# Token sums built in the down inputs' tiles, padding tiles of 160 and 352 bytes, and quarter weights that begin 480 bytes into longer tiles

## The chip, the cores and the metric

The kernel runs on one core of one Trainium2 chip. The metric is the device time of one execution in microseconds (us), the median over several runs. Before the change the median of 3 runs is 1138.71 us (1138.31 to 1138.89).

The engines of a core are named as the profile names them: PE is TensorE, the matrix engine (PEld is its loading of weights, which overlaps the matmuls); DVE is VectorE; ACT is ScalarE; POOL is GpSimd; SP is the engine that issues most of the transfers here. SBUF is the on-chip memory of 128 partitions from which PE reads both operands of a matmul: the *stationary* operand (the weights, 128 x 128) and the *moving* operand (128 partitions by 256 or 512 columns, one column after the other). PSUM is the memory that holds its results.

## The reference

A decoder trunk of two layers on 512 tokens of width 1024, in float32. Layer 0 mixes the tokens with a gated delta rule in 6 heads, layer 1 with sliding-window attention in 12 heads; both also attend to 256 memory tokens with 4 heads. Each layer then has an output projection and a SwiGLU feed-forward part of width 2816. Cut to what matters:

```python
for layer in range(DEPTH):                       # 2 layers
    h = rms_norm(x, ln_mix[layer])
    ...                                          # memory keys and values; mixer of the layer; queries mem_q
    mem_o = memory_attention(mem_q, mem_k, mem_v)
    x = x + jnp.concatenate([mix_out, mem_o], axis=-1) @ w_out[layer]
    x = x + swiglu(rms_norm(x, ln_ffn[layer]), w_gate_up[layer], w_down[layer])
    ...                                          # after layer 0: the K and V shared by layer 1
return rms_norm(x, ln_final)

def swiglu(h, w_gate_up, w_down):
    gu = h @ w_gate_up                           # 512 x 1024 times 1024 x 5632
    return (jax.nn.silu(gu[..., :D_FF]) * gu[..., D_FF:]) @ w_down
```

## The kernel before

Everything is held transposed: 128 features on the partitions, the 512 tokens (T) along a row, so that the 1024 features are 8 tiles (KD). P is 128, D is 1024, T is 512, and a float32 has 4 bytes.

**Products.** A float32 product is made of three matmuls of a faster type, float32r. Each operand is split into a high part, which ACT copies (`copy`, L140), and a low part, which DVE subtracts (`tt`, L153; `split` calls both). `mm3` then issues, for one 128 x 128 block of weights, high by high, high weight by low input, and low weight by high input (all L146). In the profile a group such as `pj<-ac8l,whi` reads: into PSUM tile `pj`, from moving operand `ac8l` and stationary operand `whi`.

**Weights.** `weight` loads a block of up to 128 x 1024 into a tile `wraw` by SP (L179) and splits it into a pair `whi`, `wlo` of the pool `wpool`, three pairs in turn. The tiles are all [P, D], that is 4096 bytes in each partition.

**The feed-forward part** (`ffn`) has 22 blocks of 128 hidden features in two halves of 11. The first blocks of a half are computed directly: `gate`, `projected`, with 512-column matmuls. The other gate and up products go in pairs of blocks through `quarters`: the 2 x 2 block product of Strassen's kind in Winograd's form with 7 products in place of 8, each of 12 matmuls of 256 columns. Of the 84 matmuls of one such step 48 have as moving operand a sum of quarters of the input (tiles `T`, groups `g<-T,whi` and `g<-T,wlo`) and 36 a quarter of the input itself (`g<-h,...`, `g<-l,whi`). There are 38 steps: 19 in each layer. Each product takes the next place of `ring`: a half of one of the three `whi`/`wlo` pairs, 512 elements.

**The sums.** `token_sums` makes the sums for `quarters`, four calls in each layer (j = 0 to 3) while the first gates run. A call computes four 128 x 256 sums with DVE (L1251 and L156) into one tile `raw` [P, D] and splits it through `weight` into two of eight tiles `T` [P, D], with one ACT and one DVE instruction over 1024 columns.

**Down.** After 11 hidden blocks their activations (8 pairs `h`, `l` of another pool, and 3 pairs `ac8` to `ac10` of the pool `fp`) are multiplied by the down weights, 33 matmuls of 512 columns for each of 8 output tiles (a *row*). In the second half of layer 1 the last two rows are taken in halves of 256 tokens (the *tail*), and the weights of the last one then lie in `T` tiles.

**Attention parts.** `mq0`, `mq1` are the pairs that hold the output of the memory attention of layer 0, and are the moving operand of 48 matmuls in its output projection. `oh`, `ol` are weights of the output projection of layer 1 (the *own* weights), loaded early into a pool of its attention `sp`; 48 matmuls use them.

**Where tiles lie.** Each pool hands out addresses in the order in which its tiles are first asked for, so a tile put in between moves those behind it. The kernel writes down no addresses; they follow from sizes and order. The order of instructions on each engine is set by a scheduler from the data and buffers that each waits for.

Of the kernel before, what the change touches and what calls it, by code (L numbers as in the profile page):

```python
# [9 lines left out]
F32 = mybir.dt.float32  # L10
F32R = mybir.dt.float32r
# [7 lines left out]
P = 128  # L19
T = 512  # L20
D = 1024
# [6 lines left out]
FT = DFF // P  # L28
# [58 lines left out]
class Builder:  # L87
# [94 lines left out]
    def weight(self, src, eng=None, raw=None, parts=1, pool=None, tags=("whi", "wlo"), bufs=3, after=None):  # L182

        raw = self.load(src) if raw is None else raw
        n = raw.shape[1]
        hi = self.t(pool or self.wpool, [P, D], F32R, tags[0], bufs)[:, :n]
        lo = self.t(pool or self.wpool, [P, D], F32R, tags[1], bufs)[:, :n]
        for i in range(parts):
            s = slice(i * n // parts, (i + 1) * n // parts)
            self.split(raw[:, s], hi[:, s], lo[:, s], eng or self.weng)  # L190
            if after is not None:
                for ins, other in zip((self.copied, self.low), after):
                    self.nosync(ins, other)
        return hi, lo

    def mm3(self, ps, w, k, act, start, stop, more=False):

        (wh, wl), (ah, al) = w, act
        s = slice(k * P, (k + 1) * P)
        self.head = self.mm(ps, wh[:, s], ah, start, False, more)  # L200
        self.mm(ps, wh[:, s], al, False, False, more)
        self.last = self.mm(ps, wl[:, s], ah, False, stop, more)
# [289 lines left out]
    def gates(self, ep):  # L492
        nc, a = self.nc, self.a
        ab = self.t(ep, [P, T], F32, "ab")
        self.copy(ab, self.ab)
        pt = self.bank("g")
        sel = self.consts[:, C_SEL:C_SEL + 12]
        for c in range(NC):
            self.mm(pt[:, c * 12:(c + 1) * 12], ab[:, c * P:(c + 1) * P], sel)
        pv = pt[:, 0:48].rearrange("p (c e) -> p e c", e=12)  # L500
        z = self.t(ep, [P, 12, NC], F32, "z")
        self.copy(z[:, 0:H, :], pv[:, 0:H, :])
        self.tt(nc.vector, z[:, H:, :], pv[:, H:, :],
                self.small[:, 6:12].unsqueeze(2).to_broadcast([P, H, NC]), ALU.add)
        l = self.t(ep, [P, 12, NC], F32, "l")
        self.stt(l, z, -1.0, z, ALU.mult, ALU.max)
        self.fn(l, l, AF.Exp, scale=-1.0)
        self.softplus = self.fn(l, l, AF.Ln, bias=self.one)

        self.lnb = self.t(self.mpool, [P, H, NC], F32, "lnb")  # L510
        self.stt(self.lnb, z[:, 0:H, :], 0.0, l[:, 0:H, :], ALU.min, ALU.subtract)
        ea = self.t(ep, [P, H], F32, "ea")
        self.fn(ea, self.small[:, 0:6], AF.Exp)
        g = self.gate[:, :NH].rearrange("p (h c) -> p h c", c=NC)
        self.stt(g, z[:, H:, :], 0.0, l[:, H:, :], ALU.max, ALU.add)
        self.stt(g, g, -1.0, ea.unsqueeze(2).to_broadcast([P, H, NC]), ALU.mult, ALU.mult)
        g2 = self.gate[:, :NH]
        pg = self.bank("g")
        self.mm(pg[:, 64:64 + P], self.gate, self.U)
        self.mm(pg[:, 0:NH], self.U, g2)  # L520
        self.mm(pg[:, NH:2 * NH], self.ones, g2)
        row = self.t(ep, [NH, P], F32, "row")
        self.copy(row, pg[:NH, 64:64 + P])
        dr = self.t(self.dpool, [1, NH * P], F32, "dr")
        nc.sync.dma_start(dr.rearrange("o (n i) -> (o n) i", i=P), row)
        self.dr = dr
        self.ngc = self.t(self.mpool, [P, NH], F32, "ngc")
        self.ts(self.ngc, pg[:, 0:NH], -1.0, ALU.mult)
        self.negc = self.t(self.mpool, [P, NH], F32, "negc")
        self.fn(self.negc, pg[:, 0:NH], AF.Exp)  # L530
        self.ts(self.negc, self.negc, -1.0, ALU.mult)
        self.egl = self.t(self.mpool, [P, NH], F32, "egl")
        self.fn(self.egl, pg[:, NH:2 * NH], AF.Exp)
        self.glc = self.t(self.mpool, [P, NH], F32, "glc")
        self.tt(nc.vector, self.glc, pg[:, NH:2 * NH], self.ngc, ALU.add)
# [15 lines left out]
    def gdn(self, gp):  # L551
# [56 lines left out]
        f = self.t(gp, [P, 3, NH], F32, "f")  # L608
# [10 lines left out]
        for h in range(H):  # L619
            d = DT[h]  # L620
            for c in range(NC):
                i = h * NC + c
# [18 lines left out]
        def memory_queries(m):  # L641
            mq.append(self.pair(self.mpool, f"mq{m}"))
            qm.append(self.t(self.mpool, [P, T], F32, f"qm{m}"))
            self.copy(qm[m], self.normed(4 * H + m))

        for h in range(H):
            t = self.t(gp, [P, T], F32, "qv", 5)
# [7 lines left out]
        self.use(LN_EXP)  # L655
        scores = [self.scores(gp, qm[0], self.memK[0], False)]
        memory_queries(1)
        X, every_t = self.base_inverse(gp, base_in, known)
        Tt = [every_t[:, h * NC:(h + 1) * NC, :] for h in range(H)]
# [434 lines left out]
    def ffn(self, fp, xp, layer, h, apool, rope=False):  # L1094
# [1 line left out]
        nc, a = self.nc, self.a  # L1096
        acc = self.acc
        half = FT // 2
        acts, sums, open_pairs, places, waiting = [], [], [], [], []

        col = lambda f, up: a["wgu"][layer, 2 * f + up]

# [14 lines left out]

        def put(u):
            n = len(acts)
            acts.append(self.pair(apool) if n < KD else self.pair(fp, f"ac{n}"))  # L1120
            self.split(u, *acts[-1])

        def ring():

            if not places:
                for _ in range(3):
                    two = [self.t(self.wpool, [P, D], F32R, t, 3) for t in ("whi", "wlo")]
                    places.extend(tuple(x[:, i * T:(i + 1) * T] for x in two) for i in range(2))
            places.append(places.pop(0))
            return places[-1]  # L1130

        def begin(f, up, by, tag, bufs, then):

            o = [self.t(fp, [P, T], F32, tag, bufs) for _ in range(2)]
            steps = self.quarters(fp, [col(f + i, up) for i in range(2)], sums, by, o, ring)
            next(steps)
            while waiting:
                x = waiting.pop()
                self.nosync(self.fn(x, x, AF.Silu), self.held)
            end()  # L1140
            next(steps)
            open_pairs.append((steps, then, o))
            return o

        def end():
            if open_pairs:
                steps, then, o = open_pairs.pop()
                next(steps, None)
                for x in o:
                    then(x)  # L1150
# [8 lines left out]
        for f0 in (0, half):  # L1159
# [4 lines left out]
            u = self.t(fp, [P, T], F32, "fu", 3)  # L1164
            self.tt(nc.vector, u, list(up)[-1], g, ALU.mult)
            put(u)
            for f in range(f0 + 1, f0 + half, 2):
                if f == 1:
# [26 lines left out]
        if tail < KD:  # L1195
# [9 lines left out]
            for t in parts:  # L1205
                acc = self.acc[:, t]
                for m in range(tail, KD):
                    ps, x = self.bank("pj")[:, :T // 2], self.x[m][:, t]
# [6 lines left out]
                    if seeded:  # L1215
                        x = ps
# [21 lines left out]
    def token_sums(self, fp, layer, j, h):  # L1238


        nc, q = self.nc, T // 2
        if j == 0:
            self.minus = self.t(fp, [P, 4], F32, "minus")
            self.ts(self.minus, self.gains[:, G_FFN[layer] + 4:G_FFN[layer] + 8], -1.0, ALU.mult)
        g0, g1 = (self.gain(G_FFN[layer], j + i) for i in (0, 4))
        n1 = self.minus[:, j:j + 1]
        x0, x1 = self.x[j], self.x[j + 4]
        c = self.t(fp, [P, q], F32, "fc")
        raw = self.t(fp, [P, D], F32, "raw")
        t = [raw[:, i * q:(i + 1) * q] for i in range(4)]  # L1250
        ins = nc.vector.tensor_scalar(out=c, in0=x0[:, q:], scalar1=g0, scalar2=None, op0=ALU.mult).ins  # L1251
        if layer and j:

            self.nosync(ins, self.ended)
        self.stt(t[0], x0[:, :q], g0, c, ALU.mult, ALU.subtract)
        self.stt(t[1], x1[:, q:], n1, t[0], ALU.mult, ALU.subtract)
        self.stt(t[2], x1[:, q:], g1, c, ALU.mult, ALU.subtract)
        self.stt(t[3], x1[:, :q], n1, t[1], ALU.mult, ALU.subtract)
        hl = self.weight(None, raw=raw, pool=fp, tags=("T", "T"), bufs=8)
        parts = {f"t{i + 1}": [x[:, i * q:(i + 1) * q] for x in hl] for i in range(4)}  # L1260
        parts["11"] = [x[:, :q] for x in h[j]]
        parts["21"], parts["22"] = ([x[:, i * q:(i + 1) * q] for x in h[j + 4]] for i in range(2))
        return parts
# [123 lines left out]
    def swa(self, sp):  # L1387
# [97 lines left out]
        for t in range(6):  # L1485
            score(t)
            work, n = (queries(t + 2), (2, 3, 4)) if t < 4 else (rows[t - 4], (1, 1, 2))
# [8 lines left out]
        settle(*beside(5, some(rows[3], 2), some(rows[4], 3), (next(rows[m]) for m in (4, 4, 4, 0, 1))))  # L1496
        for m in range(2, 5):
            list(some(rows[m], 1))
        return mix, rows

    def final(self, fp, acc, x, o, t, width):
# [105 lines left out]
```

## Time and profile before

| | before |
|---|---|
| median of 3 runs | 1138.71 us (1138.31 to 1138.89) |
| the profiled execution | 1139.05 us |
| its span | 1136.9 us |
| granted TensorE clock, mean | 0.998 |
| PE busy | 1127.1 us (99%), 7339 matmuls |
| DVE busy | 828.7 us (73%), 1545 instructions |
| ACT busy | 635.1 us (56%), 1277 instructions |
| POOL busy | 73.1 us (6%), 91 instructions |

The span runs from the first to the last instruction that the profiler saw; the execution's own time is 2.15 us longer. Where two matmuls follow each other without a wait, the second one starts before the end of the first is recorded, so durations overlap; what a matmul costs is the distance from its start to the start of the next one. A timeline row gives the start, the duration, the engine and the instruction, and `x2` stands for two neighbours of one kind in one row. In the groups the columns after the bar are the busy time of the group in us and the mean of one instruction in ns.

The stages that matter below, by the start times of their matmuls in the profiled execution: output projection of layer 0 up to 318.7 us; feed-forward part of layer 0 with quarter products at 318.7 to 406.8 and 479.6 to 577.6 us, and down rows at 406.8 to 474 and 577.6 to 644 us; projections and attention of layer 1 to 767 us, its output rows to 783 us; first gates of its feed-forward part to 805.7 us, quarter products to 893.7 and from 966 to 1064.5 us, down rows at 893.7 to 961 and 1064.5 to 1114 us; the tail to 1127 us, and the last store.

### The profile page before, as it was taken

To read this page: it belongs to the slowest core of one execution; us is meant where nothing else is said; L and a number is where in the kernel's file an instruction comes from. 1 tells how busy PE (TensorE), PEld (TensorE's weight loads), DVE (VectorE), ACT (ScalarE), POOL (GpSimd) and SP (SyncE) were. 2 spreads that over 40 slices of the span, in tenths; PEclk is the share of its full clock that TensorE was granted. 3 is DMA by queue.
4 is the path that set the end of the run, shared out by engine and by line. 5 is a ranking of instruction groups with operands and counts; after the bars stand their busy time and mean duration, and the time that the engine had idled before them with its cause. 6 is when DMAs were issued, how large, how long until landed. Compare 5 with 4: busy or idle time off the path is not lost.

```text
span 1136.9 us, 19317 instructions
## 1 busy us (share of the span) xinstructions
PE 1127.1 (99%) x7339; PEld 991.7 (87%) x7339; DVE 828.7 (73%) x1545; ACT 635.1 (56%) x1277; POOL 73.1 (6%) x91
## 2 busy tenths in 40 slices
PE   9999999999999999999999999999999999999997
PEld 8888778887899988899988887788999988999986
DVE  7676976577888975588955877839999533889643
ACT  8588664566566632366643555956666322666434
POOL 0000000000011001011000000000112000111000
PEclk9999999999999999999999999999999999999999
DMA  8344252234567536377533321116587533676232
GB/s 312 112 149 149 93 130 85 84 121 148 172 162 189 140 108 176 102 179 193 135 88 102 130 74 38 56 39 191 147 195 188 142 101 105 172 190 155 77 102 86
DMA packets 72399, 151.14 MB, mean 133 GB/s; under 512 B 16956, under 2 KB 18516, under 8 KB 72308
## 3 DMA queue, kind: packets, MB, share of 16 engines
q1 hardware_dynamic: 60884, 129.21, 36.0%
q0 software_dynamic: 11136, 20.45, 11.0%
q8 instruction: 57, 0.93, 0.3%
q14 instruction: 34, 0.28, 0.1%
q10 hardware_dynamic: 288, 0.26, 0.1%
HBM read 142.94 MB, written 6.96 MB: 132 GB/s over the span
## 4 chain that ended last, share of the span: by engine, by line
PE 96%; DVE 2%; ACT 1%; DMA 0%; issue 0%; SPq 0%; DVEq 0%; ACTq 0%
PE pj L146 46%; PE g L146 38%; PE sc L146 6%; PE qk L146 3%; PE pt L146 2%; PE pt L150 1%; PE g L150 1%; DVE big L153 1%; DMA early<-in_early 0%; DVE qv L156 0%; DVE btmp L153 0%; DVE wlo L153 0%; ACT sm L134 0%; ACT whi L140 0%; DVE T L153 0%
## 5 line engine op out<-in xcount | busy, mean ns | idle before, releaser
L140 ACT ACTIVATE whi<-wraw 128x512 fp32r<-128x512 f32 (+3 forms) x318 | 235.8, 749 | 254.1 <-PE pj L146 170.5
L153 DVE TENSOR_TENSOR wlo<-wraw,whi 128x512 fp32r<-128x512 f32 (+3 forms) x318 | 263.5, 839 | 92.3 <-ACT whi L140 84.7
L146 PE MATMUL pj<-h,whi 128*128 128x512 f32 (+1 forms) x652 | 256.4, 395 | 0.0
L146 PE MATMUL pj<-l,whi 128*128 128x512 f32 (+1 forms) x652 | 254.4, 390 | 0.0
L146 PE MATMUL pj<-h,wlo 128*128 128x512 f32 (+1 forms) x652 | 254.0, 390 | 0.0
L146 PE MATMUL g<-T,whi 128*128 128x256 f32 x1216 | 218.5, 280 | 0.0
L146 PEld LDWEIGHTS g<-T,whi 128*128 128x128 f32 x1216 | 186.1, 188 | 1.2 <-DVE fu L156 1.2
L146 PE MATMUL g<-T,wlo 128*128 128x256 f32 x608 | 170.1, 280 | 0.0
L146 PEld LDWEIGHTS pj<-h,whi 128*128 128x128 f32 x652 | 122.4, 188 | 28.2 <-issue 4.1
L146 PE MATMUL g<-h,wlo 128*128 128x256 f32 (+1 forms) x500 | 146.1, 292 | 0.0
L146 PE MATMUL g<-l,whi 128*128 128x256 f32 (+1 forms) x500 | 146.0, 292 | 0.0
L146 PE MATMUL g<-h,whi 128*128 128x256 f32 (+1 forms) x500 | 145.6, 291 | 0.0
L146 PEld LDWEIGHTS pj<-h,wlo 128*128 128x128 f32 x652 | 122.5, 188 | 25.3 <-issue 0.9
L146 PEld LDWEIGHTS pj<-l,whi 128*128 128x128 f32 x652 | 122.7, 188 | 23.9 <-DVE l L1458 0.3
L146 PEld LDWEIGHTS g<-T,wlo 128*128 128x128 f32 x608 | 114.3, 188 | 0.0
L146 PEld LDWEIGHTS g<-l,whi 128*128 128x128 f32 x500 | 95.0, 190 | 2.0
L146 PEld LDWEIGHTS g<-h,whi 128*128 128x128 f32 x500 | 94.9, 190 | 2.0
L146 PEld LDWEIGHTS g<-h,wlo 128*128 128x128 f32 x500 | 95.1, 190 | 1.7
L1276 POOL DMA_DIRECT2D ws<-in_wgu x38 | 33.6, 885 | 747.9 <-DMA ws<-in_wgu 586.7
L140 ACT ACTIVATE whi<-ws 128x512 fp32r<-128x512 f32 x76 | 48.0, 632 | 46.7 <-PE g L146 38.0
L153 DVE TENSOR_TENSOR wlo<-ws,whi 128x512 fp32r<-128x512 f32 x76 | 52.1, 686 | 6.9 <-ACT whi L140 6.8
L1277 POOL DMA_DIRECT2D ws<-in_wgu x38 | 34.5, 909 | 188.7 <-DVE wlo L153 80.0
(401 smaller groups left out, 1684.6 us busy)
## 6 DMA issues: line engine op xcount, KB each, us to landing
wraw<-in_wgu SPq DMA_DIRECT2D x50, 512.0 KB, 4.2
ws<-in_wgu SPq DMA_DIRECT2D x76, 256.0 KB, 3.5
ws<-in_wgu POOLq DMA_DIRECT2D x76, 256.0 KB, 4.7
wraw<-in_win SPq DMA_DIRECT2D x26, 512.0 KB, 3.7
wraw<-in_wdn SPq DMA_DIRECT2D x32, 384.0 KB, 3.0
wraw<-in_wdn SPq DMA_DIRECT2D x32, 320.0 KB, 2.9
wraw<-in_wgu SPq DMA_DIRECT2D x38, 256.0 KB, 4.1
wraw<-in_wout SPq DMA_DIRECT2D x16, 512.0 KB, 3.5
```

The source lines that it names most:

```text
L140: self.copied = self.nc.scalar.activation(out, in_, AF.Copy, **kw).ins
L146: return self.nc.tensor.matmul(out, lhsT, rhs, start=start, stop=stop, skip_group_check=more).ins
L150: return self.nc.tensor.transpose(out, in_, self.ident[:k, :k]).ins
L153: return eng.tensor_tensor(out=out, in0=a, in1=b, op=op).ins
L1276: nc.gpsimd.dma_start(s1, a22, accum_op=ALU.add)
L1277: nc.gpsimd.dma_start(s3, a21, accum_op=ALU.add)
```

## The change

The order and the shapes of all matmuls stay as they are. What changes is where operands lie in SBUF, and how `token_sums` holds and splits its sums.

- The `whi` and `wlo` tiles of `wpool` become [P, D + P], 4608 bytes in place of 4096. In `ring` a place is now 640 elements long, and once `begin` has run for the first time the quarter weights lie P - 8 = 120 elements (480 bytes) into it. Other weights still begin at a tile's start.
- `token_sums` no longer has its tile `raw`. It writes its four sums into the tiles of one of the pairs `ac8`, `ac9`, `ac10` (j modulo 3), and each tile of 512 columns is split by itself: two ACT and two DVE instructions over 512 columns in place of one each over 1024. In both layers together that is 8 more instructions on ACT and 8 more on DVE.
- Tiles that nothing reads or writes are put into pools: `gap` with 88 elements (352 bytes) ahead of `lnb` in the pool `mpool`; `rest` with 40 elements (160 bytes) behind `qm1` in `mpool`, ahead of the last down input in `fp`, and at the end of the attention in `sp`.

```diff
-        hi = self.t(pool or self.wpool, [P, D], F32R, tags[0], bufs)[:, :n]
-        lo = self.t(pool or self.wpool, [P, D], F32R, tags[1], bufs)[:, :n]
+        hi, lo = (self.part(tag, bufs, pool)[:, :n] for tag in tags)
...
+    def part(self, tag, bufs=3, pool=None):
+        return self.t(pool or self.wpool, [P, D if pool else D + P], F32R, tag, bufs)
...
+        self.t(self.mpool, [P, 88], F32, "gap")
         self.lnb = self.t(self.mpool, [P, H, NC], F32, "lnb")
...
             qm.append(self.t(self.mpool, [P, T], F32, f"qm{m}"))
+            if m:
+                self.t(self.mpool, [P, 40], F32, "rest")
...
         def put(u):
             n = len(acts)
+            if n == FT // 2 - 1 and not sized:
+                sized.append(self.t(fp, [P, 40], F32, "rest"))
...
                 for _ in range(3):
-                    two = [self.t(self.wpool, [P, D], F32R, t, 3) for t in ("whi", "wlo")]
-                    places.extend(tuple(x[:, i * T:(i + 1) * T] for x in two) for i in range(2))
+                    two = [self.part(tag) for tag in ("whi", "wlo")]
+                    places.extend(tuple(x[:, i * T:(i + 1) * T + P] for x in two) for i in range(2))
             places.append(places.pop(0))
-            return places[-1]
+            return [x[:, shift[0]:shift[0] + T] for x in places[-1]]
...
             steps = self.quarters(fp, [col(f + i, up) for i in range(2)], sums, by, o, ring)
+            shift[0] = P - 8
             next(steps)
...
-        raw = self.t(fp, [P, D], F32, "raw")
-        t = [raw[:, i * q:(i + 1) * q] for i in range(4)]
+        raws = [self.t(fp, [P, T], F32, f"ac{8 + j % 3}{n}") for n in "hl"]
+        t = [raws[i // 2][:, i % 2 * q:(i % 2 + 1) * q] for i in range(4)]
...
-        hl = self.weight(None, raw=raw, pool=fp, tags=("T", "T"), bufs=8)
+        hl = [self.t(fp, [P, D], F32R, "T", 8) for _ in range(2)]
+        for i, raw in enumerate(raws):
+            self.split(raw, *(x[:, i * T:(i + 1) * T] for x in hl))
...
         for m in range(2, 5):
             list(some(rows[m], 1))
+        self.t(sp, [P, 40], F32, "rest")
         return mix, rows
```

**What moves in SBUF.** The table gives, for the matmuls whose operands move, the byte address within a partition modulo 64 of the moving operand and of the weights, as the built kernels place them. All addresses that matmuls read are multiples of 32 bytes, so each is 0 or 32.

| matmuls | columns | number | before: moving, weights | after: moving, weights |
|---|---|---|---|---|
| quarter products on sums `T` | 256 | 1824 | 32, 0 | 0, 32 |
| quarter products on `h`, `l` | 256 | 1368 | 0, 0 | 0, 32 |
| down inputs `ac8` to `ac10` | 512 | 270 | 32, 0 | 0, 0 |
| `mq0`, `mq1` in the output of layer 0 | 512 | 48 | 32, 0 | 0, 0 |
| own weights `oh`, `ol` of layer 1 | 512 | 48 | 0, 32 | 0, 0 |
| tail, `h`, `l` by weights in `T` | 256 | 48 | 0, 32 | 0, 0 |
| tail, `ac8` to `ac10` by weights in `T` | 256 | 18 | 32, 32 | 0, 0 |
| tail, `ac8` to `ac10` by `whi`, `wlo` | 256 | 18 | 32, 0 | 0, 0 |
| attention of layer 1 on `pf` and `ks` | 128, 256 | 264 | 32, 0 and 0, 32 | 0, 32 and 32, 0 |
| other float32 matmuls of attention: `consts`, `mk`, `m0`, `m1`, `pfm` | 128 to 512 | 212 | 0, 32 or 32, 32 | 0, 0 |

The other 2160 matmuls of 512 columns by `whi`, `wlo` have 0, 0 before and after; some twenty small moves are left out. Taken modulo 128 the weights of a quarter product lie 96 bytes past the moving operand, before and after, where that operand is a sum `T`; where it is `h` or `l`, the distance is 0 before and 96 after. In the tail by weights in `T` on `h`, `l` it is 32 before.

**What moves in order.** On PE the sequence of instructions is the same. On SP three loads stand one or two places later: one `wraw` of the feed-forward part of layer 0, a `ws` and a `wraw` of that of layer 1. On DVE (and on ACT beside it) the order changes around the sums.

The first place is DVE at the start of the feed-forward part of layer 1, around the end of the second sum (j = 1). `x_...` are the input tiles, `minus`, `gains` and `fc` operands of the sums, `T_...` the low parts of the split sums, `wlo_8329` (before) and `wlo_8354` (after) the low part of the third gate weight, `fg` a gate. Before:

```order
L156 SCALAR_TENSOR_TENSOR raw_8271<-x_522_2730,minus_8257,raw_8271 128x256
L153 TENSOR_TENSOR wlo_8329<-wraw_8326,whi_8328 128x1024
L153 TENSOR_TENSOR T_8278<-raw_8271,T_8277 128x1024
L153 TENSOR_TENSOR fg_8230<-pj_8180,rstd_2741 128x512
L156 SCALAR_TENSOR_TENSOR raw_8316<-x_519_2727,gains_67,fc_8315 128x256
```

After, from the same instruction on:

```order
L156 SCALAR_TENSOR_TENSOR ac9l_8291<-x_524_2732,minus_8273,ac9h_8290 128x256
L156 SCALAR_TENSOR_TENSOR ac10h_8338<-x_521_2729,gains_67,fc_8337 128x256
L153 TENSOR_TENSOR T_8298<-ac9h_8290,T_8297 128x512
L156 SCALAR_TENSOR_TENSOR ac10h_8338<-x_525_2733,minus_8273,ac10h_8338 128x256
L153 TENSOR_TENSOR T_8298<-ac9l_8291,T_8297 128x512
L153 TENSOR_TENSOR fg_8246<-pj_8196,rstd_2743 128x512
L156 SCALAR_TENSOR_TENSOR ac10l_8339<-x_525_2733,gains_67,fc_8337 128x256
L156 SCALAR_TENSOR_TENSOR ac10l_8339<-x_525_2733,minus_8273,ac10h_8338 128x256
L153 TENSOR_TENSOR T_8346<-ac10h_8338,T_8345 128x512
L153 TENSOR_TENSOR wlo_8354<-wraw_8351,whi_8353 128x1024
```

The split of the second sum is two instructions of 512 columns with a sum of the third call between them, and the third gate weight's low part stands eight instructions further back: behind the second sum's split, a gate and the first part of the third sum's split.

The second place is DVE some instructions on, where the last sum (j = 3) is finished and the first quarter weights are split (`ws`, `wraw` are their sources). Before:

```order
L153 TENSOR_TENSOR wlo_8386<-ws_8374,whi_8385 128x512
L156 SCALAR_TENSOR_TENSOR raw_8360<-x_524_2732,minus_8257,raw_8360 128x256
L153 TENSOR_TENSOR wraw_8372<-ws_8374,wraw_8372 128x512
L153 TENSOR_TENSOR wlo_8388<-wraw_8372,whi_8387 128x512
L153 TENSOR_TENSOR T_8367<-raw_8360,T_8366 128x1024
```

After:

```order
L153 TENSOR_TENSOR wlo_8414<-ws_8402,whi_8413 128x512
L153 TENSOR_TENSOR fg_8334<-pj_8309,rstd_2743 128x512
L156 SCALAR_TENSOR_TENSOR ac8l_8386<-x_526_2734,minus_8273,ac8h_8385 128x256
L153 TENSOR_TENSOR T_8393<-ac8h_8385,T_8392 128x512
L153 TENSOR_TENSOR wraw_8400<-ws_8402,wraw_8400 128x512
L153 TENSOR_TENSOR T_8393<-ac8l_8386,T_8392 128x512
```

The first half of the last split comes ahead of the sum of two weights in `wraw`, the second half behind it, and the next weight's split, which came before the whole of it, now follows both.

More of the change, by code (lines that the diff above doesn't have):

```diff
@@ L1098, in ffn @@
         half = FT // 2
-        acts, sums, open_pairs, places, waiting = [], [], [], [], []
+        acts, sums, open_pairs, places, waiting, shift, sized = [], [], [], [], [], [0], []
         col = lambda f, up: a["wgu"][layer, 2 * f + up]
```

## The prediction

> **What bounds the kernel now.** I read the page's busy times first, then its chain of work that ended last, by engine and by line, then what PE waits for.
>
> ```profile
> PE 1127.1 (99%) x7339; PEld 991.7 (87%) x7339; DVE 828.7 (73%) x1545; ACT 635.1 (56%) x1277; POOL 73.1 (6%) x91
> PE 96%; DVE 2%; ACT 1%; DMA 0%; issue 0%; SPq 0%; DVEq 0%; ACTq 0%
> PE g L146 <- DVE eps L292: 1.2, 1, 1.2
> PE pj L146 <- ACT whi L140: 0.5, 1, 0.5
> PE g L146 <- DVE DT L153: 0.4, 1, 0.4
> ```
>
> PE is busy for 99% of the span and is 96% of the chain, and its three waits sum to 2.1 us. There is nothing left to hide, and the change keeps every matmul, so the time can move only in two ways: the distance between the starts of matmuls changes, or one of the moved instructions elsewhere comes so late that PE waits. The first needs evidence that a distance depends on where operands lie. The PE timeline of a down row has it.
>
> ```profile
> 413.77 0.40 PE L146 MATMUL pj<-ac8h,whi 128*128 128x512 f32 x1
> ...
> 415.88 0.39 PE L146 MATMUL pj<-h,whi 128*128 128x512 f32 x1
> ...
> 421.32 0.40 PE L146 MATMUL pj<-ac8h,whi 128*128 128x512 f32 x1
> ```
>
> The row's first 9 matmuls read `ac8` to `ac10`, the other 24 `h` and `l`; shape, weights pool and PSUM tile are the same. The 9 take 2.11 us, 234.4 ns each; the 24 take 5.44 us, 226.7 ns each. The former have places 32, 0 (moving, weights, modulo 64), the latter 0, 0. The groups agree:
>
> ```profile
> L146 PE MATMUL pj<-ac9l,whi 128*128 128x512 f32 x30 | 12.0, 400 | 0.0
> L146 PE MATMUL g<-h,whi 128*128 128x512 f32 x44 | 17.1, 389 | 0.0
> ```
>
> [...]
>
> **The change part by part.**
>
> *Quarter products, 3192 matmuls of 256 columns.* One step of 84 runs from 498.11 to 508.05 us:
>
> ```profile
> 489.56 0.40 PE L146 MATMUL g<-T,whi 128*128 128x256 f32 x2
> ...
> 493.83 0.28 PE L146 MATMUL g<-h,whi 128*128 128x256 f32 x1
> ...
> 496.70 0.40 PE L146 MATMUL g<-T,whi 128*128 128x256 f32 x2
> ...
> 498.11 0.28 PE L146 MATMUL g<-h,whi 128*128 128x256 f32 x1
> ...
> 499.53 0.40 PE L146 MATMUL g<-T,whi 128*128 128x256 f32 x2
> ...
> 503.76 0.28 PE L146 MATMUL g<-h,whi 128*128 128x256 f32 x1
> ...
> 508.05 0.28 PE L146 MATMUL g<-h,whi 128*128 128x256 f32 x1
> ```
>
> That is 9.94 us, 118.3 ns each. Runs of one kind differ: 36 on `T` from 499.53 take 4.23 us, 117.5 each; 36 on `T` from 489.56 take 4.27, 118.6 each; 24 on `h`, `l` from 493.83 take 2.87, 119.6 each. So places 32, 0 are better here than 0, 0, which at 512 columns was the other way round, and even one pair of places has two spacings. The groups carry the same in their means:
>
> ```profile
> L146 PE MATMUL g<-T,whi 128*128 128x256 f32 x1216 | 218.5, 280 | 0.0
> L146 PE MATMUL g<-h,wlo 128*128 128x256 f32 x456 | 128.8, 283 | 0.0
> ```
>
> After, all 3192 have places 0, 32. That pair is seen at 256 columns only in the tail, on 24 matmuls:
>
> ```profile
> 1115.28 0.28 PE L146 MATMUL pj<-h,T 128*128 128x256 f32 x1
> ...
> 1118.16 0.28 PE L146 MATMUL pj<-ac8h,T 128*128 128x256 f32 x1
> ```
>
> 2.88 us, 120.0 each. So the trace has two neighbours. The sums' operands lie 96 bytes apart modulo 128 before and after, and the change brings `h` and `l` to 96 as well: by the distance all go at 117.5. By the pair of places they go at the tail's 120.0, where the distance is 32. I take the distance: 1824 of the 3192 keep it exactly, their weights and inputs merely exchange which of them lies on the odd 32 bytes, and at 512 columns that exchange matters little (234.4 above against 233.3 for the own weights below). Then 3192 x 117.5 ns = 375.1 us against 38 x 9.94 = 377.7, a gain of 2.7. The ends: at 120.0 they are 383.0, a loss of 5.3; at half of 233.3 ns, 116.7, they would be 372.4, a gain of 5.3.
>
> *Down inputs.* 270 matmuls come to 0, 0: 30 rows, each 2.11 - 9 x 0.2267 = 0.07 us shorter: -2.1. Ends: 0 and -2.1.
>
> *Memory outputs and own weights.*
>
> ```profile
> 268.83 0.40 PE L146 MATMUL g<-mq0h,whi 128*128 128x512 f32 x1
> ...
> 274.36 0.40 PE L146 MATMUL pj<-mq0h,whi 128*128 128x512 f32 x1
> ...
> 296.47 0.39 PE L146 MATMUL pj<-h,whi 128*128 128x512 f32 x1
> ...
> 301.91 0.39 PE L146 MATMUL g<-h,whi 128*128 128x512 f32 x1
> ...
> 748.26 0.39 PE L146 MATMUL qk<-h,oh 128*128 128x512 f32 x1
> ...
> 752.46 0.71 PE L150 MATMUL pt<-consts,sm 128*128 128x128 f32 x5
> ```
>
> An output row of 24 with `mq0`, `mq1` in it takes 5.53 us, 24 matmuls without them 5.44. Eight rows at 0.09 give -0.7; 48 matmuls at 7.7 ns give -0.4; I take -0.5. Eighteen on own weights take 4.20 us, 233.3 each, 6.6 above 226.7: 48 of them, -0.3. Both lie on PE's path.
>
> *Tail.* 84 matmuls come to 0, 0, where `h`, `l` took 119.6 in place of 120.0: under 0.1, taken as nothing.
>
> *Attention in float32.* 476 small matmuls move, 264 of them between 32, 0 and 0, 32, and 212 to 0, 0. No row isolates them. At the own weights' 6.6 ns the 212 would be worth -1.4; a loss of the same size is not excluded. I take 0, since these matmuls are short and of other shapes, and keep 1.4 either way.
>
> *The sums' splits.*
>
> ```profile
> L153 DVE TENSOR_TENSOR T<-raw,T 128x1024 fp32r<-128x1024 f32 x8 | 9.8, 1222 | 0.0
> L153 DVE TENSOR_TENSOR wlo<-wraw,whi 128x512 fp32r<-128x512 f32 x190 | 128.0, 689 | 17.1 <-ACT whi L140 12.3
> L140 ACT ACTIVATE T<-raw 128x1024 fp32r<-128x1024 f32 x8 | 8.5, 1057 | 1.8 <-DVE raw L156 1.7
> L140 ACT ACTIVATE whi<-wraw 128x512 fp32r<-128x512 f32 x190 | 117.3, 628 | 70.6 <-PE g L146 47.7 <-PE pj L146 19.1 <-ACT fs L140 2.6
> ```
>
> Two of 689 ns in place of one of 1222 add 0.16 us on DVE per sum, two of 628 for 1057 add 0.2 on ACT, 0.6 and 0.8 us per layer. What has to cover it is seen at the start of layer 1's feed-forward part:
>
> ```profile
> 791.62 1.22 DVE L153 TENSOR_TENSOR wlo<-wraw,whi 128x1024 fp32r<-128x1024 f32 x1
> 800.21 0.39 PE L146 MATMUL pj<-h,whi 128*128 128x512 f32 x1
> 804.02 1.22 DVE L153 TENSOR_TENSOR T<-raw,T 128x1024 fp32r<-128x1024 f32 x1
> 807.09 0.40 PE L146 MATMUL g<-T,whi 128*128 128x256 f32 x2
> ```
>
> The third gate weight's low part was ready at 792.84, and its gate begins on PE at 800.21, 7.4 us later. It now stands behind eight more DVE instructions; three splits of 0.7, a gate of about 0.7 and the rest of 256 columns make it some 4 us later, which leaves 3.4. ACT's high part of that weight and the first gate, both queued behind the same sums, have that cover too. The last sum was ready at 805.24, 1.85 us before the first product on sums, so 0.6 us more on DVE still fits. Cost taken: 0. If the cover were gone, each microsecond of lateness is one of PE.
>
> *Loads.* POOL's queue is unchanged. Of SP's three moved loads the one of layer 0 is the nearest to its reader:
>
> ```profile
> 298.84 0.33 SPq L179 DMA_DIRECT2D wraw<-in_wgu  x1
> 307.85 0.62 ACT L140 ACTIVATE whi<-wraw 128x512 fp32r<-128x512 f32 x1
> ```
>
> Two more issues of 0.4 us and the landing, 4.2 us in the page's list of transfers, end at 304, before 307.85. Cost 0. The unused tiles cost no instruction.
>
> **Sum.** -2.7 - 2.1 - 0.5 - 0.3 = -5.6 us. The profiled execution took 1139.05 us, its span 1136.9 plus 2.15 around it, and comes to 1133.4; it is 0.34 above the median, so the median comes to 1133.1. That forecast's own range is 1131.7 to 1134.5, by attention.
>
> **The rivals.**
>
> *Quarter products at the tail's spacing.* The pair 0, 32 decides and not the distance: +5.3 - 2.9 = +2.4 us, 1141.1, slower. It has the only rows with that pair for it; against it, they are one short stretch. It decides from where the quarter products lose more than the 2.9 gained elsewhere, 118.3 + 0.9 = 119.2 ns on average.
>
> *Quarter products all at the sums' second spacing*, 118.6, as in the run from 489.56: 378.6 us, +0.9 - 2.9 = -2.0, so 1136.7. For it: the trace shows that one pair of places settles in two ways. Against: most sums show 117.5, or a step would not come to 118.3.
>
> *Places do nothing.* The distances come from something else, say the start of an accumulation, since `ac8` to `ac10` always come first in a row. Then the time stays at 1138.7. Against it, the spacing changes at 415.88, ten matmuls into the row, just when the operand does, and own weights show 233.3 without being a row's first. [...]
>
> *A new stall of DVE* at the start of layer 1's feed-forward part. If the last sum came 4 us later as the third weight does, PE would wait 4 - 1.85 = 2.2 us: 1135.3.
>
> **Chances.** Forecast 0.50, tail's spacing 0.28, second spacing 0.14, new stall 0.05, places do nothing 0.03. A difference of 0.2%, 2.3 us, is about what this kernel's measurement can tell. Faster: forecast and stall, 0.55. Same: second spacing and no effect, 0.17. Slower: tail's spacing, 0.28. For the range the upper end has the tail's case and half of attention's 1.4, 1141.8. The lower end has the quarter products at 116.7, 372.4 us, -5.3 - 2.9 = 1130.5, less attention's 1.4: 1129.0.
>
> **What would show it.** In the changed profile a down row's 33 matmuls should take 7.48 us throughout, an output row of layer 0 5.44, the own weights 226.7 ns each. A quarter step should take 84 x 117.5 = 9.87 us with no difference between runs on `T` and on `h`; 10.08 shows the tail's spacing, 9.96 the second one. PE's waits should stay near 2.1 us; a new one on a `T` or a `wlo` of DVE near 800 us is the stall. What would make me wrong above all is that the spacing of 256-column matmuls follows a rule that these two neighbours do not show.

## The result and the profile after

The changed kernel takes 1130.91 us (median of 4 runs, 1130.61 to 1131.37), the kernel before beside it 1138.62 us. The ratio is 0.9932, with a 95% interval from 0.992 to 0.9945. That is 7.7 us faster. The forecast was a gain of 5.6 us and 1133.1 us, with a range of 1129.0 to 1141.8, and the result lies inside it. The sign and the place of the gain came as forecast; the term of the quarter products was half of what it turned out to be.

The page after (busy times, chain by engine) and PE's waits:

```profile
PE 1119.9 (99%) x7339; PEld 986.1 (87%) x7339; DVE 827.6 (73%) x1553; ACT 634.4 (56%) x1285; POOL 73.2 (6%) x91
PE 96%; DVE 2%; ACT 1%; DMA 0%; issue 0%; DVEq 0%; SPq 0%; ACTq 0%
PE g L146 <- DVE eps L294: 1.2, 1, 1.2
PE g L146 <- DVE DT L153: 0.4, 1, 0.4
PE pj L146 <- ACT mh L140: 0.2, 1, 0.2
```

PE is as full as before and waits for 1.8 us in place of 2.1, so the 7.5 us by which the span is shorter (1129.4 against 1136.9) lie in the distances between matmuls. The eight more instructions on DVE and on ACT are there (1553 for 1545, 1285 for 1277).

The PE timeline of the same 33 down matmuls, of the same 24 matmuls with `mq0` and `mq1`, and of the 18 on own weights:

```profile
268.89 0.39 PE L146 MATMUL g<-mq0h,whi 128*128 128x512 f32 x1
...
274.33 0.39 PE L146 MATMUL pj<-mq0h,whi 128*128 128x512 f32 x1
...
412.16 0.39 PE L146 MATMUL pj<-ac8h,whi 128*128 128x512 f32 x1
...
414.20 0.39 PE L146 MATMUL pj<-h,whi 128*128 128x512 f32 x1
...
419.64 0.39 PE L146 MATMUL pj<-ac8h,whi 128*128 128x512 f32 x1
...
744.38 0.39 PE L146 MATMUL qk<-h,oh 128*128 128x512 f32 x1
...
748.47 0.71 PE L150 MATMUL pt<-consts,sm 128*128 128x128 f32 x5
```

The 9 matmuls on `ac8` to `ac10` now take 2.04 us, 226.7 ns each, as do the 24 on `h` and `l` behind them; the 33 take 7.48 us. The 24 with `mq0`, `mq1` take 5.44 us in place of 5.53, the 18 on own weights 4.09 in place of 4.20.

The same quarter step, whose runs on `T` and on `h` differed before:

```profile
495.65 0.28 PE L146 MATMUL g<-h,whi 128*128 128x256 f32 x1
...
497.05 0.40 PE L146 MATMUL g<-T,whi 128*128 128x256 f32 x2
...
501.25 0.28 PE L146 MATMUL g<-h,whi 128*128 128x256 f32 x1
...
505.45 0.28 PE L146 MATMUL g<-h,whi 128*128 128x256 f32 x1
```

It takes 9.80 us, 116.7 ns each, in place of 9.94: the 36 on `T` from 497.05 take 4.20 us, and the remaining 48 take 5.60, also 116.7 each.

Where the gain lies, from the starts of all matmuls of a kind in the two traces (a kind's sum of distances to the next start):

| matmuls | before, us | after, us | change | forecast |
|---|---|---|---|---|
| quarter products on `T`, 1824 | 214.9 | 213.2 | -1.7 | |
| quarter products on `h`, `l`, 1368 | 163.2 | 159.6 | -3.6 | |
| all quarter products | 378.2 | 372.8 | -5.4 | -2.7 |
| down inputs, 270 | 63.1 | 61.2 | -1.9 | -2.1 |
| memory outputs and own weights, 96 | 23.8 | 23.3 | -0.5 | -0.8 |
| everything else | | | +0.2 | 0 |
| sum | | | -7.6 | -5.6 |

What is left is the size of the first term: why 116.7 ns, where the sums had shown 117.5 and 118.6, and the tail 120.0.

### The profile page after: what moved, and what is told of

Read it like the earlier page. It is cut to its first block, busy times and chain, and to the rows that moved or that the text cites. A ratio compares the mean times of both kernels' runs of the same rounds, so it can differ in the third digit from the quotient of the medians.

```text
span 1129.4 us, 19330 instructions
## 1 busy us (share of the span) xinstructions
PE 1119.9 (99%) x7339; PEld 986.1 (87%) x7339; DVE 827.6 (73%) x1553; ACT 634.4 (56%) x1285; POOL 73.2 (6%) x91
## 4 chain that ended last, share of the span: by engine, by line
PE 96%; DVE 2%; ACT 1%; DMA 0%; issue 0%; DVEq 0%; SPq 0%; ACTq 0%
PE pj L146 46%; PE g L146 38%; PE sc L146 6%; PE qk L146 3%; PE pt L146 2%; PE pt L150 1%; PE g L150 1%; DVE big L153 1%; DVE qv L156 0%; DVE btmp L153 0%; DMA early<-in_early 0%; DVE wlo L153 0%; ACT sm L134 0%; DVE T L153 0%; DVE gcr L153 0%
```

## The experiments

Two theories of the quarter products' spacing stood beside each other first: the pair of places modulo 64 decides, or the distance between weights and moving operand does, modulo 128 or more. In all runs the sequence of matmuls is the same; in all but run 3 only the start of the weights, or of the sums and down inputs, moves.

**1. The quarter weights at the start of their places.**

```diff
-            shift[0] = P - 8
+            shift[0] = 0
```

> The changed kernel, with the quarter weights at the start of their places (0 in place of 480 bytes); everything else stays. All 3192 quarter matmuls then have places 0, 0 with distance 0. Theory (the place of the weights sets the spacing): they go back to the 119.3 to 120.0 ns that quarter matmuls on h and l showed in the kernel before, 380.8 to 383.0 us in place of 372.5, so 1139 to 1141.5 us. Rival (what cost time before was the alternation between two pairs of places, and any one pair for all is as good): 116.7 ns stay, 1130.9 us.

Measured: 1141.17 us, ratio 1.0021 to the kernel before (1.0012 to 1.0030). The same step:

```profile
498.10 0.28 PE L146 MATMUL g<-h,whi 128*128 128x256 f32 x1
...
508.18 0.28 PE L146 MATMUL g<-h,whi 128*128 128x256 f32 x1
```

10.08 us, 120.0 ns each, on sums as on `h`. All quarter products take 383.3 us, 10.5 more than after the change, and the time is 10.3 more. So one pair for all is not enough, and with this one place undone the rest of the change ends slower than the kernel before: at distance 0 the quarter products lose more (383.3 us for 378.2 before) than the 512-column matmuls gain (2.4 us in the table).

**2. The quarter weights 32 bytes in.** The same line with `shift[0] = 8`.

> The changed kernel, with the quarter weights 32 bytes into their places in place of 480. Places modulo 64 are 0, 32 as in the changed kernel, but the distance modulo 128 is 32 in place of 96. Theory A (the pair of places modulo 64 decides): 116.7 ns stay, 1130.9 us. Theory B (the distance of 96 decides, as the prediction argued, and the tail's 120.0 ns before belonged to the distance of 32): 120.0 ns, 3192 x 3.3 ns = 10.5 us more, 1141.4 us.

Measured: 1136.10 us, ratio 0.9975 (0.9965 to 0.9985); the step:

```profile
496.70 0.28 PE L146 MATMUL g<-h,whi 128*128 128x256 f32 x1
...
506.64 0.28 PE L146 MATMUL g<-h,whi 128*128 128x256 f32 x1
```

118.3 ns each, between both theories. The places modulo 64 are those of the changed kernel with its 116.7, so they do not decide alone; but the distance of 32 does not give the tail's 120.0 either.

**3. The new token sums alone**, on the kernel before, with the old tile still asked for so that no place modulo 64 changes.

```diff
-        raw = self.t(fp, [P, D], F32, "raw")
-        t = [raw[:, i * q:(i + 1) * q] for i in range(4)]
+        self.t(fp, [P, D], F32, "raw")
+        raws = [self.t(fp, [P, T], F32, f"ac{8 + j % 3}{n}") for n in "hl"]
+        t = [raws[i // 2][:, i % 2 * q:(i % 2 + 1) * q] for i in range(4)]
...
-        hl = self.weight(None, raw=raw, pool=fp, tags=("T", "T"), bufs=8)
+        hl = [self.t(fp, [P, D], F32R, "T", 8) for _ in range(2)]
+        for i, raw in enumerate(raws):
+            self.split(raw, *(x[:, i * T:(i + 1) * T] for x in hl))
```

> The kernel before with the new token sums alone: the sums stand in the tiles of ac8 to ac10 and each is split in two parts, while the tile of the old sums is still asked for and left unused, so that no operand of a matmul changes its place modulo 64. Theory (the covers of 1.8 us and more hold): the time of the kernel before, 1138.6 us within 0.6, and PE's waits near 2 us. Rival (the later split makes PE wait in the first gates of layer 1): up to 2.2 us more, 1140.8 us, with a wait of PE on a T or a wlo of DVE.

Measured: 1138.65 us, ratio 0.9996 (0.9987 to 1.0005). The groups are those of before:

```profile
L146 PE MATMUL g<-T,whi 128*128 128x256 f32 x1216 | 218.5, 280 | 0.0
L146 PE MATMUL g<-h,wlo 128*128 128x256 f32 x456 | 128.8, 283 | 0.0
L146 PE MATMUL pj<-ac9l,whi 128*128 128x512 f32 x30 | 12.0, 400 | 0.0
```

The splits cost nothing that can be measured (the interval is 1 us either way), so the gain is in the places.

**4. Another start in each step.** `shift[0]` and the start of the down weights are taken from lists, so that one trace shows 30 distances at 256 columns and 17 at 512.

```diff
-            shift[0] = P - 8
+            shift[0] = moved.pop(0) // 4
...
+                move = downs.pop(0) // 4
...
-                    w = down(m, j, n)
+                    w = down(m, j, n, move=move)
```

> The changed kernel, with another start of the weights in each quarter step (38 steps of 84 matmuls, 0 to 256 bytes into the place) and in each down row (30 rows, 0 to 512 bytes), while the moving operands stay on multiples of 64. Read by step, not by the total. Theory A: the mean spacing depends on the weights' start modulo 64 alone; 256 columns 116.7 ns at 32, 160, 224 as at 96, and about 119.5 at multiples of 64; 512 columns 226.7 at multiples of 64 and 233 at odd multiples of 32. Theory B: at 256 columns 116.7 only at 96 and 224, and 120.0 at 32 and 160. Starts of 16 bytes and less that are no multiple of 32 were never seen; if only 32-byte steps count, they show one of these values, and otherwise something between or worse.

Neither theory holds. The spacing changes from start to start, also between those that are no multiple of 32, and some starts have two. Steady values in ns for some of the starts, by the distance in bytes modulo 256 (the moving operands stay on one place modulo 256), together with run 6:

| distance | 256 columns | distance | 256 columns | distance | 512 columns |
|---|---|---|---|---|---|
| 0 | 120.0 | 88 | 113.3 | 0 | 226.7 |
| 4 | 118.3 | 96 | 117.3 or 118.7 | 16 | 226.7 |
| 8 | 115.6 | 108 | 122.2 | 32 | 233.2 |
| 28 | 116.7 | 112 | 120.0 | 44 | 230.1 |
| 32 | 118.3 | 160 | 120.0 | 96 | 233.9 |
| 48 | 123.3 | 172 | 116.7 | 100 | 226.7 |
| 52 | 113.3 | 204 | 123.3 | 120 | 227.0 |
| 64 | 117.8 | 208 | 116.7 | 160, 224 | 233.4 |
| 76 | 113.3 | 224 | 116.7 or 117.8 | 164 | 238.0 |

The down rows of layer 0 took 0 to 224 bytes and then 256 to 480, and the second eight repeated the spacings of the first within 0.1 ns, so modulo 256 fits there.

Here lie the numbers that stood apart: before the change the sums had the distance 96 modulo 256 (117.5 and 118.6 ns), `h` and `l` 0 (120.0 once settled), the tail 160 (120.0), own weights 160 and down inputs 96 at 512 columns (233.3 and 234). After it all quarter products have 224. Two steps of this run at 224 settled differently:

```profile
386.55 0.28 PE L146 MATMUL g<-h,whi 128*128 128x256 f32 x1
...
395.03 0.40 PE L146 MATMUL g<-T,whi 128*128 128x256 f32 x2
...
558.78 0.28 PE L146 MATMUL g<-h,whi 128*128 128x256 f32 x1
...
567.18 0.40 PE L146 MATMUL g<-T,whi 128*128 128x256 f32 x2
```

In both 72 matmuls at distance 224: 8.48 us, 117.8 each, behind a step at 192 bytes, and 8.40 us, 116.7 each, behind one at 40. A third step at 224 changed on its way. It comes first in layer 1, behind the same gates as in the changed kernel:

```profile
807.20 0.28 PE L146 MATMUL g<-h,whi 128*128 128x256 f32 x1
...
810.00 0.40 PE L146 MATMUL g<-T,whi 128*128 128x256 f32 x2
...
814.24 0.40 PE L146 MATMUL g<-T,whi 128*128 128x256 f32 x2
```

The first 24 take 2.80 us, 116.7 each, as all do in the changed kernel; the 36 from 810.00 take 4.24 us, 117.8 each. The change falls where the third product begins, whose weights lie in the next place of `ring`; the distance modulo 256 is the same. In the changed kernel nothing changes there: 116.7 before and behind it. One thing differs between the two: in runs 4, 6 and 9 the places of a weights tile lie 576 elements apart in place of 640, that is 256 bytes nearer.

**5. 52 bytes throughout**, since the step there was the shortest: `shift[0] = 13`.

> The changed kernel, with the quarter weights 52 bytes into their places in place of 480. In the run with another start in each step the one step at 52 bytes settled at 113.3 ns, the shortest of all. Theory (the distance between weights and moving operand, modulo 256, sets the spacing, step after step): 3192 x (116.7 - 113.3) = 10.6 us less than the changed kernel, 1120.3 us. Rival (that step's spacing was its place in the order or its moment): 116.7 ns and more, 1130.9 us or above.

Measured: 1140.86 us, ratio 1.0016 (1.0006 to 1.0025). Of its 10 executions one took 1136.29 us, the others 1140.5 to 1141.4; the short one was not profiled. The step, in one of the others:

```profile
498.40 0.28 PE L146 MATMUL g<-h,whi 128*128 128x256 f32 x1
...
508.48 0.28 PE L146 MATMUL g<-h,whi 128*128 128x256 f32 x1
```

120.0 ns from the first step to the last. The theory missed, by 20 us: the distance modulo 256 alone does not fix the spacing.

**6. The remaining multiples of 4 bytes**, with 52, 8 and 224 once more; the edit of run 4 with other lists.

> As the first run with another start in each step, at the remaining multiples of 4 bytes: 256 columns at 68 to 252, and 52, 8 and 224 once more; 512 columns in the down rows at 12 to 252. Theory (distance modulo 256, with no shorter period): every start has a spacing of its own, between 113 and 124 ns, 52 gives 113.3 and 8 gives 115.6 again, and 512 columns lie between 226.7 and 234, with perhaps a shorter one below 32 bytes' grid. Rival (modulo 64): 68 to 124 repeat 4 to 60, so 116 repeats 113.3 ns and 112 the 123.3 of 48.

52 bytes gave 113.3 again, twice, 60 matmuls in 6.80 us as in run 4 (the first pair is run 4's):

```profile
1008.34 0.39 PE L146 MATMUL g<-T,whi 128*128 128x256 f32 x2
...
1015.14 0.39 PE L146 MATMUL g<-T,whi 128*128 128x256 f32 x2
```

```profile
1028.38 0.39 PE L146 MATMUL g<-T,whi 128*128 128x256 f32 x2
...
1035.18 0.39 PE L146 MATMUL g<-T,whi 128*128 128x256 f32 x2
```

And 8 gave 115.6 again. Modulo 64 does not hold: 116 showed 118.6 to 119.2 where 52 showed 113.3, and 112 showed 120.0 where 48 showed 123.3. Whole kernels with distances that are equal modulo 64 say the same: 118.3 at 32 (run 2), 117.3 at 96 (run 8) and 116.7 at 224 (the changed kernel). At 512 columns no start went below 226.7, but the upper bound of 234 missed: 164 bytes took 238.0, 212 bytes 236.2. So 52 bytes has at least two steady patterns: 113.3, found behind steps at 44, 252 and 8 bytes, and 120.0, found behind the first gates, whose 512-column matmuls have distance 0. The first was seen only with places 576 elements apart, the second only with 640.

**7. Sums and down inputs on odd multiples of 32, at distance 224.** Quarter weights at the start of their places, and the unused tile in `put` 96 elements long in place of 40.

> The changed kernel, with the quarter weights at the start of their places and the unused tile ahead of the last down input longer by 224 bytes, so that the sums and the down inputs lie on odd multiples of 32 as before the change. Quarter products on sums have places 32, 0 as before, but the distance is 224 modulo 256, where it was 96; those on h and l have 0, 0 and the distance 0; down inputs 32, 0 and 224. Theory (only the distance modulo 256 counts, not which operand lies on the odd 32): the sums show the spacings of the distance 224, 116.7 or 117.8 ns, h and l 119 to 120, down inputs 233. Rival (places count): the sums show the 117.5 and 118.6 of before.

One execution: 1139.89 us. Sums 117.8 to 118.3 ns, `h` and `l` 119.4 to 120.0; as an example 36 on `T`, then 24 on `h`:

```profile
489.35 0.40 PE L146 MATMUL g<-T,whi 128*128 128x256 f32 x2
...
493.59 0.28 PE L146 MATMUL g<-h,whi 128*128 128x256 f32 x1
...
496.47 0.40 PE L146 MATMUL g<-T,whi 128*128 128x256 f32 x2
```

4.24 us, 117.8 each, and 2.88 us, 120.0 each. The down inputs, at 224 too, took 233.4 each on average. The 117.8 is one of the two spacings of the distance 224, here on the places 32, 0; but it also lies between the two that the sums showed before, so the run fits the theory without deciding it. It does show that sums at the changed kernel's distance do not by themselves have its 116.7 while `h` and `l`, at 0, alternate with them.

**8. 96 bytes throughout**: `shift[0] = 24`, the distance that the sums had before, for all.

> The changed kernel, with the quarter weights 96 bytes into their places in place of 480: the distance is 96 modulo 128 as in the changed kernel, and modulo 256 it is 96, as the sums had before the change, against 224. Theory (modulo 256): 117.5 or 118.6 ns, the two spacings of the sums before, for all 3192, which is 2.7 to 6 us more than the changed kernel, 1133.5 to 1137. Rival (modulo 128, as the prediction reasoned): 116.7 ns, 1130.9 us.

Measured: 1132.96 us, ratio 0.9946 (0.9929 to 0.9962); the kernel before took 1139.18 us beside it.

```profile
495.94 0.28 PE L146 MATMUL g<-h,whi 128*128 128x256 f32 x1
...
505.80 0.28 PE L146 MATMUL g<-h,whi 128*128 128x256 f32 x1
```

9.86 us, 117.3 ns each, and 375.0 us for all quarter products. Modulo 128 the kernel is like the changed one, and its quarter products take 2.2 us longer. That speaks for modulo 256, though both the spacing and the time lie a little below what the theory gave.

**9. Another first step.** The first quarter step of each half at 8 bytes, all others at 52.

```diff
-            shift[0] = P - 8
+            shift[0] = 13 if open_pairs else 2
```

> The changed kernel, with the quarter weights 8 bytes into their places in the first quarter step of each half and 52 bytes in all later ones. At 52 bytes from the start on, the matmuls settled at 120.0 ns and stayed there; behind steps at other distances (8, 44 and 252) they settled at 113.3. Theory (the distance allows several steady patterns, and the one that is in force when the distance begins decides, and then stays): the 4 primed steps take 115.6 to 118 ns, the other 34 take 113.3: about 10 us less than the changed kernel, 1121 us. Rival (113.3 was an accident of those runs): 120.0 at 52 bytes, 1140 us.

Measured: 1121.80 us (4 runs, 1121.48 to 1122.17), ratio 0.9848 (0.9833 to 0.9862).

```profile
492.34 0.28 PE L146 MATMUL g<-h,whi 128*128 128x256 f32 x1
...
501.86 0.28 PE L146 MATMUL g<-h,whi 128*128 128x256 f32 x1
```

9.52 us, 113.3 ns each, where run 5 had 120.0 with the same places in the same step. The four first steps took 115.6; the others held 113.3 to the end of their halves. In one of them, at 816.4 us, two matmuls came late by 0.2 us together, and some ten matmuls later 113.3 was back. Run 5 and run 9 differ by 19 us, and in two things: these four steps, and 256 bytes between the two halves of a weights tile. No run has 52 bytes from the start in the tiles of run 9, so which of the two decides is not shown. That 0, 8, 32 and 96 bytes showed the same spacing in both kinds of tiles (120.0, 115.6, 118.3 and 117.3; 96 also 118.7 in one) speaks for the four steps. That 224 behind the same gates kept 116.7 in one kind and went to 117.8 in the other speaks against them. This version beats both kernels: 9.1 us less than the changed one.

**10. 8 bytes throughout**: `shift[0] = 2`.

> The changed kernel, with the quarter weights 8 bytes into their places in all steps. In the two runs with another start in each step, 8 bytes gave 115.6 ns both times, behind different steps. Theory (a distance with one steady pattern): 115.6 ns from the start, 3192 x 1.1 = 3.5 us less than the changed kernel, 1127.4 us. Rival (it has a second pattern, as 52 bytes had): 117.8 to 120 ns, 1134 to 1141 us.

Measured: 1127.30 us, ratio 0.9896 (0.9881 to 0.9910).

```profile
494.09 0.28 PE L146 MATMUL g<-h,whi 128*128 128x256 f32 x1
...
503.79 0.28 PE L146 MATMUL g<-h,whi 128*128 128x256 f32 x1
```

115.6 ns from the first step on, behind the same gates after which 52 bytes settled at 120.0. At this distance no second pattern showed.

## Why the prediction was right, and where a term was off

- *PE bounds, and only distances and new stalls can move the time.* Right: waits 1.8 us after, 2.1 before, and the parts in the table add up to the change. The rival that places do nothing is out: runs 1 and 9, whose matmul operands differ in the start of the quarter weights alone, would take the same time by it, and they are 19.4 us apart (1141.17 and 1121.80).
- *The down row that the reasoning began with* was read wrongly in one point. A row does not begin with `ac8` to `ac10`, it ends with them. The first row of the kernel before, with the last twelve quarter products among its first matmuls:

```profile
406.80 0.39 PE L146 MATMUL pj<-h,whi 128*128 128x512 f32 x1
...
413.77 0.40 PE L146 MATMUL pj<-ac8h,whi 128*128 128x512 f32 x1
...
415.88 0.39 PE L146 MATMUL pj<-h,whi 128*128 128x512 f32 x1
```

  So the nine matmuls end one row and the 24 behind them begin the next, with another PSUM tile. At 415.88 the operand and the row change together, and the argument drawn from that moment against the rival *places do nothing* does not hold. The result does: in the same order the nine take 226.7 ns as well.
- *Down inputs, memory outputs, own weights.* Right: -1.9 for -2.1, -0.24 for -0.3 on own weights, and for the memory outputs -0.24 in the table and -0.44 in all for -0.5. Five of the eight groups are rows like the one at 268.83; each fell from 5.53 to 5.44 us. Half of that is in the six matmuls on `mq0` and `mq1`, the other half in the nine on `h` and `l` behind them, which took 231.4 ns each before and 226.7 after, though their own places stayed. The other three groups, among matmuls of the mixer, gained 0.005 to 0.008 us each in their six matmuls.
- *Attention in float32, taken as 0.* Right: 476 moved matmuls changed by less than 0.1 us together.
- *Splits, third gate weight, loads, taken as covered.* Right, by run 3. The profile after shows how the cover stood:

```profile
791.47 1.21 DVE L153 TENSOR_TENSOR wlo<-wraw,whi 128x1024 fp32r<-128x1024 f32 x1
795.99 0.39 PE L146 MATMUL pj<-h,whi 128*128 128x512 f32 x1
799.39 0.68 DVE L153 TENSOR_TENSOR T<-ac8l,T 128x512 fp32r<-128x512 f32 x1
802.84 0.40 PE L146 MATMUL g<-T,whi 128*128 128x256 f32 x2
```

  The third gate weight was ready at 792.68, 3.3 us before its gate, where 3.4 were forecast. The last sum was ready at 800.07, 2.8 us before the first product on sums: more than the 1.85 of before, not less, with the next weight's split, which came ahead of it, now behind it.
- *Quarter products.* The step that was mis-sized is the term "3192 x 117.5 ns = 375.1 us": measured 372.8, 116.7 each. The reasoning chose the distance over the pair of places, which was the better of the two, but took it modulo 128 and held that the sums keep theirs "exactly". Modulo 256 they go from 96 to 224, and that 224 was no worse was luck. Run 8 is the kernel that the reasoning described, all at 96: it took 375.0 us for these products and 1132.96 us in all, against 375.1 and 1133.1 forecast. The second neighbour, the tail's 120.0, was a row of the distance 160, which run 4 also shows at 120.0, and said nothing on 224.
- *The rival of the second spacing* foresaw that one pair of places settles in two ways, and gave it 0.14. That is real, and larger than thought: 113.3 and 120.0 ns at 52 bytes. The changed kernel's 224 has two as well (116.7 and 117.8), and settles on the shorter from its first product on; had it taken the other, it would be 3192 x 1.1 ns = 3.5 us slower.

How much of the change's gain on sums is the new distance and how much the end of the alternation with `h` and `l` at distance 0 is not fully separated: on average over all 1824, sums in alternation took 117.8 ns at 96 (before) and 118.2 at 224 (run 7), and unmixed 117.6 at 96 (run 8) and 116.9 at 224 (after). So on these runs the end of the alternation is worth 0.2 ns at 96 and 1.3 at 224, and the new distance alone, in the mix, nothing.

## What to carry to other kernels

Where PE is full, compare the start-to-start distance of matmuls of one shape between the groups of a timeline: if it differs, as 226.7 and 234.4 ns did here, the operands' addresses are worth a trial, and one run that takes another start in each repetition prices many of them at once. A spacing that such a run finds must be tried from the start in the real sequence, since the same distance settled in two ways here (113.3 and 120.0 ns at 52 bytes); where it settles badly, a few matmuls at another distance ahead of it, or tiles laid out otherwise, are worth a run, as run 9, which did both, showed (1121.80 us against 1140.86). Do not infer an address rule from two neighbours, and write down the period (64, 128, 256) that an argument assumes.

## What the runs showed of the hardware

The spacing of back-to-back float32r matmuls, with a weights load for each, depended in these runs on where weights and moving operand lie in SBUF: from 113.3 to 123.3 ns at 256 columns and from 226.7 to 238.0 at 512, with a granted clock of 0.998 to 0.999 in the profiled executions. Both operands counted: before the change, weights at a tile's start took 226.7 ns in the down rows with `h` and `l` and 233.7 with `ac8` to `ac10`. That only the distance between them counts fits all the rows, but most runs moved the weights alone, and run 7 did not decide it. Steps of 4 bytes mattered (120.0 ns at 0, 118.3 at 4), and neither 64 nor 128 is the period (113.3 at 52, 118.6 to 119.2 at 116; 118.3 at 32, 120.0 at 160); 256 fits the down rows, which repeated within 0.1 ns.

Unexpected was that one distance can settle in two ways: at 52 bytes 120.0 ns lasted from the first quarter step to the last in run 5, and 113.3 in run 9 from the second step of each half to its end, but for some ten matmuls. What chooses between them is open. A step at 8 bytes ahead goes with the shorter one in run 9, but so do places 256 bytes nearer to each other, and at 224 bytes, in such tiles, the spacing once changed from 116.7 to 117.8 ns in the middle of a step. Why these distances are good is open too; nothing in the profile shows what a matmul waits for between two starts.
